# HGRN2's halving levels two at a time, both heads of a pair at the same steps, from copied queries

## The chip, the cores and the metric

One NeuronCore of one Trainium2 chip runs the whole program; the other cores are idle. The metric is the device time of one execution, in microseconds (us): 1566.15 us, the median of 3 runs (1566.15 to 1567.37). Lower is better.

The core has five engines with a program each: TensorE (PE, matrix products), VectorE (DVE), ScalarE (ACT), GpSimd (POOL) and SyncE (SP, which starts the loads). Each takes its instructions in the order in which they stand, and they wait for each other by semaphores. PEld is TensorE's loading of weights, beside its products.

## The reference, cut to what matters

The model has two layers, on 512 tokens of 1024 channels. The first mixes tokens by HGRN2, the second by Mamba-2; after each comes a gated feed-forward with a short convolution. The change touches HGRN2 alone: for each of 8 heads of 128 channels and in both directions it computes a gated recurrence.

```python
def gla_chunked(q, k, v, logf):
    """S_t = diag(f_t) S_{t-1} + k_t v_t^T, o_t = S_t^T q_t"""
...
def hgrn2_mixer(u, w_in, lb, norm_w, w_out):
    q, f_fw, f_bw, iv, g = jnp.split(u @ w_in, 5, axis=-1)
    f = lb + (1.0 - lb) * jax.nn.sigmoid(fr)      # k = 1 - f, logf = log(f)
    q = heads(jax.nn.silu(q))
    o = gla_chunked(q, k_fw, iv, logf_fw) + flip(gla_chunked(flip(q), flip(k_bw), flip(iv), flip(logf_bw)))
    o = rmsnorm(o, norm_w) * jax.nn.silu(heads(g))
    return o.reshape(bsz, seq, HG_DIM) @ w_out
```

The weight with which token s enters the output of token t is the product of the gates between them, channel by channel, so it is no plain matrix product.

## The kernel before, in words

Channels lie on the 128 partitions and tokens along the free side, in 4 blocks of 128. All products of weights and activations are split in halves of fewer bits (`whi`, `wlo` of the weights, `uhi`, `ulo` of the activations) and made of three matmuls each (`mm3`, lines 161 to 163). SP loads a piece of weights, ACT rounds it to `whi` (line 135), DVE makes the rest `wlo` (line 136).

**The stream of projections.** `fill` projects the heads in four pairs: `q`, forward gate, backward gate, `v` and `g`, 16 units of work each, where a unit is about three matmuls of 512 columns. After the pairs follows `ao0`, the output product over the first six heads.

**The heads' own work.** `mix(hd)` is a generator for one head. In `kq` it keeps four 512-wide arrays: forward keys KF, backward queries QB, forward queries QF, backward keys KB. The token pairs within a block of 128 are taken by halving: at level m (1, 2, 4, 8, 16, 32, 64) the two neighbouring runs of m tokens meet. Up to m=16 a level gathers the keys that it needs into `km` (ACT, line 558) and makes 16 small products of 32x32 (`strips`, line 541) into a PSUM tile; a masked copy (DVE, line 566; for m=1 an ACT copy, line 563, and a masked copy of the diagonal, line 564, whose product has the sum `ks` of both keys, line 547, as weights) takes them into `atd`. At m=32 there are 16 products of 32x32 (line 572) and at m=64 8 of 64x64 (lines 580, 582). After each level three DVE instructions carry the gates one level up: two in place in `kq` (lines 594, 595: the later halves get one product of gates, the earlier halves the other), and one for the next products of gates `tot` (line 597). So a level's products must be done before `kq` is changed, and the next level needs the change. Then the keys are transposed (line 606), states between blocks are made (614, 619), the output is made (632), normed (636 to 641), transposed back (645), gated by `g` (647) and split (648, 649).

**What sets the order.** `weave` runs the stream and, when its count of units has come to a head's time, one step of that head's generator. A head has 13 steps, spread evenly over its span in `HEADS` by `HSTEPS`; the spans of neighbouring heads overlap, each with its own times. TensorE's instructions stand in just that order (`manual_schedule`). The order of DVE and ACT is made by the framework's scheduler from the dependencies, when the program is built. Buffers that the change touches: `q` and `g` 3, `km` 2, `y` 1, `kq` 2; PSUM has 3 tiles for the stream (`pp`) and 5 for the rest (`pm`).

Of the kernel before, what the change touches and what calls it, by code (L numbers as in the profile page):

```python
# [14 lines left out]
ALU = mybir.AluOpType  # L15
# [3 lines left out]
P = 128  # L19
Q = 32  # L20
T = 512
NB = T // P
# [8 lines left out]
NFF = DFF // P  # L31
FHALF = (12, 10)

HEADS = ((66, 136), (90, 170), (133, 209), (169, 250), (213, 292), (248, 315), (293, 353), (314, 368))
HSTEPS = (1, 1, 2, 3, 4, 5, 6, 7, 8.3, 9.5, 10, 11, 12)

MAMBA = [(c[0], int(c[1:])) for c in "p0 z0 p1 z1 p2 z2 o1 p3 o1 z3 o2 p4 z4 o2 p5 z5 o2 p6 z6 p7 z7 o8".split()]

# [13 lines left out]
def view(ap, offset, dims):  # L52

    return bass.AP(tensor=ap.tensor, offset=ap.offset + offset, ap=[ap.ap[0], *dims])
# [3 lines left out]
def tile_trunk(ctx: ExitStack, tc: tile.TileContext, x, norm1_w, norm2_w, a_w_in, a_lb_logits, a_norm_w, a_w_out,  # L58
# [3 lines left out]
    V, A, G, PE = nc.vector, nc.scalar, nc.gpsimd, nc.tensor  # L62
# [9 lines left out]
    def misc_ps():  # L72
        return ps.tile([P, T], F32, tag="pm", name="pm", bufs=5)
# [17 lines left out]
    masks = {}  # L91
# [187 lines left out]
    for step in MAMBA:  # L279
        g = step[1]  # L280
# [7 lines left out]
        else:  # L288
            for n in range(g):
                k, c = min(nout // 4 * 2, 6), nout % 4  # L290
# [118 lines left out]
    with tc.manual_schedule(engines={mybir.EngineType.PE, mybir.EngineType.DVE, mybir.EngineType.Activation}):  # L409
# [9 lines left out]
        w = halves(*raws[0])  # L419
# [8 lines left out]
        w = halves(*raws[2])  # L428
# [4 lines left out]
        w = halves(*raws[1])  # L433
# [4 lines left out]
        w = halves(*raws[3])  # L438
# [18 lines left out]
    def hgrn2():  # L457
# [5 lines left out]
        def t2k(tag, bufs, name=None):  # L463
            return pool.tile([P, T], F32, tag=tag, name=name or tag, bufs=bufs)
# [3 lines left out]
        def proj_pair(j):  # L468
            q, F = [], []
            if j > 0:  # L470
                wq = take(("a", j, 0))
            for i in range(2):
                if j == 0:
                    p = first[i]
                else:
                    p = proj_ps()
                    yield from proj_ch(p, wq, i * P)
                t = t2k("pr", 2)
                V.tensor_tensor(t, p, rbc, ALU.mult)
                s = t2k("sg_", 1)  # L480
                A.activation(s, t, AF.Sigmoid)
                q.append(t2k("q", 3))
                V.tensor_tensor(q[i], t, s, ALU.mult)
                F.append(pool.tile([P, 2, T], F32, tag="F", name="F", bufs=2))

            def gate(i, dr, w, p=None):
                if p is None:
                    p = proj_ps()
                    yield from proj_ch(p, w, i * P)
                t = t2k("pr", 2)  # L490
                V.tensor_tensor(t, p, rbc, ALU.mult)
                A.activation(t, t, AF.Sigmoid)
                hd = 2 * j + i
                V.tensor_scalar(F[i][:, dr, :], t, olb[:, hd:hd + 1], lb[:, hd:hd + 1], ALU.mult, ALU.add)
# [12 lines left out]
            for c in range(2):  # L507
                p = proj_ps()
                yield from proj_tok(p, wv, (2 * c, 2 * c + 1))
                for b in range(2):  # L510
                    A.activation(v[:, 2 * c + b, :], p[:, b * 256:(b + 1) * 256], AF.Copy,
                                 scale=rtok[:, 2 * c + b:2 * c + b + 1])
            wg = take(("a", j, 4))
            for i in range(2):
                p = proj_ps()
                yield from proj_ch(p, wg, i * P)
                t = t2k("pr", 2)
                V.tensor_tensor(t, p, rbc, ALU.mult)
                s = t2k("sg_", 1)
                A.activation(s, t, AF.Sigmoid)  # L520
                g.append(t2k("g", 3))
                V.tensor_tensor(g[i], t, s, ALU.mult)

        def mix(hd):
            q, F, v, g = heads[hd]
# [11 lines left out]
            def strips(lhs, rhs, p):  # L537

                for b in range(NB):
                    for j in range(0, P, Q):  # L540
                        PE.matmul(p[j:j + Q, b * Q:(b + 1) * Q], lhs(b * P + j), rhs(b * P + j), start=True, stop=True)

            def pq(p):
                return p[:, 0:P].rearrange("p (a b) -> p a b", b=Q)

            ks = t2k("km", 2)
            V.tensor_tensor(ks, kq[:, KF, :], kq[:, KB, :], ALU.add)
            p0 = misc_ps()
            strips(lambda o: ks[:, o:o + Q], lambda o: q[:, o:o + Q], p0)
            yield  # L550
            tot = F
            m = 1
            while m < P:
                n2 = T // (2 * m)
                pl = misc_ps()
                if m < Q:
                    km = t2k("km", 2)
                    A.copy(km.rearrange("p (a b c) -> p a b c", b=2, c=m),
                           view(kq, 0, [[2 * m, n2], [3 * T + m, 2], [1, m]]))
                    strips(lambda o: km[:, o:o + Q],  # L560
                           lambda o: view(kq, T + o, [[2 * m, Q // (2 * m)], [T + m, 2], [1, m]]), pl)
                    if m == 1:
                        A.copy(atd, pq(pl))
                        V.copy_predicated(atd, bmask(masks[0]), pq(p0))
                    else:
                        V.copy_predicated(atd, bmask(masks[m]), pq(pl))
                elif m == Q:

                    half = ((0, KF, QF, Q), (Q, KB, QB, 0), (2 * Q, KF, QF, 3 * Q), (3 * Q, KB, QB, 2 * Q))
                    for b in range(NB):  # L570
                        for j, k, r, t in half:
                            PE.matmul(pl[j:j + Q, b * Q:(b + 1) * Q], kq[:, k, b * P + j:b * P + j + Q],
                                      kq[:, r, b * P + t:b * P + t + Q], start=True, stop=True)
                    for j, k, r, t in half:
                        A.copy(pv(at0[j:j + Q])[:, :, t:t + Q], pq(pl)[j:j + Q])
                    for j in range(0, P, Q):
                        V.tensor_copy(pv(at0[j:j + Q])[:, :, j:j + Q], atd[j:j + Q])
                else:
                    for b in range(NB):
                        PE.matmul(pl[0:64, b * P + 64:b * P + 128], kq[:, KF, b * P:b * P + 64],  # L580
                                  kq[:, QF, b * P + 64:b * P + 128], start=True, stop=True)
                        PE.matmul(pl[64:128, b * P:b * P + 64], kq[:, KB, b * P + 64:b * P + 128],
                                  kq[:, QB, b * P:b * P + 64], start=True, stop=True)
                    A.copy(pv(at0[0:64])[:, :, 64:128], pv(pl[0:64])[:, :, 64:128])
                    A.copy(pv(at0[64:128])[:, :, 0:64], pv(pl[64:128])[:, :, 0:64])

                w = T // m

                def tv(half):
                    return view(tot, half, [[w, 2], [2, n2], [0, m]])  # L590

                qk2 = view(kq, QF * T + m, [[T, 2], [2 * m, n2], [1, m]])
                kq1 = view(kq, 0, [[T, 2], [2 * m, n2], [1, m]])
                V.tensor_tensor(qk2, qk2, tv(0), ALU.mult)
                V.tensor_tensor(kq1, kq1, tv(1), ALU.mult)
                nt = pool.tile([P, 2, n2], F32, tag=f"tot{m}", name=f"tot{m}", bufs=2 if m > 2 else 1)
                V.tensor_tensor(nt, view(tot, 0, [[w, 2], [2, n2]]), view(tot, 1, [[w, 2], [2, n2]]), ALU.mult)
                tot = nt
                m *= 2
                yield  # L600

            kt, blocks = [], ((0, 1, 2), (3, 2, 1))
            for a, bl in zip((KF, KB), blocks):
# [17 lines left out]
                for n, b in enumerate(bl):  # L621
                    states[dr, b + 1 - 2 * dr] = sd[:, n, :]
            yield
            yield

            po = misc_ps()
            for t in range(NB):
# [15 lines left out]
            pt = misc_ps()  # L643
            for t in range(NB):
                PE.transpose(pt[:, t * P:(t + 1) * P], on[:, t * P:(t + 1) * P], ident)
            y = t2k("y", 1)
            V.scalar_tensor_tensor(y, pt, col(W_AN, 0), g[i], ALU.mult, ALU.mult)
            A.copy(yhi[hd], y)
            V.tensor_tensor(ylo[hd], y, yhi[hd].bitcast(F32), ALU.subtract)
# [5 lines left out]
                yield from proj_pair(j)  # L655
            yield from out_proj("ao0", yhi[:6], ylo[:6], None)

        jobs = [(mix(i), [a + (b - a) * f / 13 for f in HSTEPS]) for i, (a, b) in enumerate(HEADS)]
        with tc.manual_schedule(engines={mybir.EngineType.PE}):
            weave(fill(), jobs, 32)  # L660
        run(out_proj("ao1", yhi[6:], ylo[6:], lambda d: prep(d, (W_N2[0], W_N2[1]), pool)))
# [484 lines left out]
```

## Time and profile before

| | |
|---|---|
| median of the runs | 1566.15 us |
| profiled execution, its own time | 1567.89 us |
| its span, first to last instruction | 1566.1 us |
| TensorE busy | 1544.3 us (99%) |
| VectorE busy | 1042.7 us (67%) |
| ScalarE busy | 776.9 us (50%) |
| mean granted TensorE clock | 0.995 of full |

A share of busy time says which engine is short over the whole span; a timeline row gives the start, the time of the (merged) instructions, engine, line, operation and tiles, and in brackets how long the engine was idle before it and who ended that. Matmul records overlap: a record is longer than the step to the next one. A 32x32 product of full precision leaves two records, so 16 products are a row of x32. The granted clock is given in shares of full speed, 2.4 GHz; 0.50 is the lower level, 1.2 GHz.

### The profile page before, as it was taken

The numbers are of one execution on the slowest core, as the hardware profiler recorded it, in microseconds if no ns is written. First come the engines' busy times: TensorE is split into PE (matmuls) and PEld (weight loads), VectorE is DVE, ScalarE is ACT, GpSimd is POOL, SyncE is SP. The second block draws the span as 40 slices with busy tenths as digits, with TensorE's granted clock in tenths as the row PEclk, the third lists the DMA queues.
The fourth block names the chain that finished last, engine by engine and source line by source line (L and its number), as shares of the span: only waits on it lengthen the run. The fifth ranks groups of instructions, "written<-read, shape, count | busy, mean of one in ns | idle before, by whom it ended". The sixth has DMA issues, their size and how long they took to land.

```text
span 1566.1 us, 24651 instructions
## 1 busy us (share of the span) xinstructions
PE 1544.3 (99%) x9959; PEld 1287.7 (82%) x9959; DVE 1042.7 (67%) x1675; ACT 776.9 (50%) x1382; POOL 27.2 (2%) x31
## 2 busy tenths in 40 slices
PE   8999999999999999999999999999999999999998
PEld 6878788887888888887887888888887888888887
DVE  6687778758664346645988887778978655346543
ACT  5445545435333223333698886667845333123333
POOL 0000000000000000000000000000000000000000
PEclk9999999999999999999999999999999999999999
DMA  5322221113232332323443433333313323233221
GB/s 181 95 69 69 69 82 62 56 49 127 88 108 81 108 96 93 101 88 91 129 125 114 142 103 113 122 103 114 101 48 123 106 82 107 81 108 101 81 86 70
DMA packets 153592, 151.52 MB, mean 97 GB/s; under 512 B 8374, under 2 KB 144263, under 8 KB 153479
## 3 DMA queue, kind: packets, MB, share of 16 engines
q1 hardware_dynamic: 153415, 149.93, 30.8%
q8 instruction: 78, 1.28, 0.3%
q14 instruction: 35, 0.29, 0.1%
q0 software_dynamic: 32, 0.02, 0.0%
q10 hardware_dynamic: 32, 0.01, 0.0%
HBM read 147.70 MB, written 2.23 MB: 96 GB/s over the span
## 4 chain that ended last, share of the span: by engine, by line
PE 49%; DVE 2%; ACT 1%; issue 1%; POOL 0%; POOLq 0%; ACTq 0%
PE pp L161 14%; PE pp L163 14%; PE pp L162 14%; PE pm L960 2%; PE pm L954 1%; PE pm L921 1%; PE pm L870 0%; PE pm L994 0%; PE pm L881 0%; PE pm L163 0%; PE pm L161 0%; PE pm L162 0%; PE pm L865 0%; PE pm L1075 0%; ACT whi L135 0%
## 5 line engine op out<-in xcount | busy, mean ns | idle before, releaser
L161 PE MATMUL pp<-uhi,whi 128*128 128x512 f32 x1184 | 474.7, 401 | 0.0
L163 PE MATMUL pp<-uhi,wlo 128*128 128x512 f32 x1184 | 462.6, 391 | 0.3 <-DVE wlo L136 0.3
L162 PE MATMUL pp<-ulo,whi 128*128 128x512 f32 x1184 | 462.7, 391 | 0.0
L135 ACT CAST whi<-raw 128x1024 fp32r<-128x1024 f32 (+1 forms) x258 | 260.0, 1008 | 318.4 <-PE pp L162 246.2
L136 DVE TENSOR_TENSOR wlo<-raw,whi 128x1024 fp32r<-128x1024 f32 (+1 forms) x258 | 301.5, 1170 | 152.6 <-ACT whi L135 151.8
L163 PEld LDWEIGHTS pp<-uhi,wlo 128*128 128x128 f32 x1184 | 222.8, 188 | 48.9 <-DVE wlo L136 1.2
L161 PEld LDWEIGHTS pp<-uhi,whi 128*128 128x128 f32 x1184 | 223.1, 188 | 46.1 <-issue 0.5
L162 PEld LDWEIGHTS pp<-ulo,whi 128*128 128x128 f32 x1184 | 223.3, 189 | 45.0 <-issue 0.8
L161 PE MATMUL pp<-yh,whi 128*128 128x512 f32 (+1 forms) x500 | 197.2, 394 | 0.9 <-ACT whi L135 0.9
L163 PE MATMUL pp<-yh,wlo 128*128 128x512 f32 (+1 forms) x500 | 191.8, 384 | 0.0
L162 PE MATMUL pp<-yl,whi 128*128 128x512 f32 (+1 forms) x500 | 190.7, 381 | 0.0
L161 PE MATMUL pp<-whi,uhi 128*128 128x256 f32 x384 | 111.3, 290 | 0.0
L163 PEld LDWEIGHTS pp<-yh,wlo 128*128 128x128 f32 x500 | 93.8, 188 | 20.3
L161 PEld LDWEIGHTS pp<-yh,whi 128*128 128x128 f32 x500 | 94.0, 188 | 18.9 <-ACT whi L135 1.3
L162 PEld LDWEIGHTS pp<-yl,whi 128*128 128x128 f32 x500 | 93.9, 188 | 18.8
L255 DVE TENSOR_TENSOR h<-h,pp 128x512 f32<-128x512 f32 x80 | 54.3, 685 | 81.6 <-PE pp L163 80.9
L163 PE MATMUL pp<-whi,ulo 128*128 128x256 f32 x384 | 108.6, 283 | 0.0
L162 PE MATMUL pp<-wlo,uhi 128*128 128x256 f32 x384 | 108.5, 283 | 0.0
L899 ACT ACTIVATE E<-R,col_t 128x128 f32<-128x128 f32 x256 | 81.4, 392 | 27.8 <-PE pm L954 21.9
L679 ACT ACTIVATE c<-gp,colp 128x512 f32<-128x512 f32 x44 | 35.8, 817 | 98.0 <-DVE gp L677 98.0
L681 DVE SCALAR_TENSOR_TENSOR c<-gp,colp,c 128x512 f32<-128x512 f32 x88 | 65.6, 750 | 20.8 <-ACT c L679 19.4
L161 PEld LDWEIGHTS pp<-whi,uhi 128*128 128x128 f32 x384 | 73.4, 191 | 0.9
(277 smaller groups left out, 1882.0 us busy)
## 6 DMA issues: line engine op xcount, KB each, us to landing
raw<-in_ffn_w_in_dram SPq DMA_DIRECT2D x88, 512.0 KB, 3.5
raw<-in_a_w_in_dram SPq DMA_DIRECT2D x40, 512.0 KB, 3.6
raw<-in_ffn_w_out_dram SPq DMA_DIRECT2D x40, 512.0 KB, 3.4
raw<-in_b_w_in_dram SPq DMA_DIRECT2D x32, 512.0 KB, 3.8
R<-ac_d SPq DMA_DIRECT2D x64, 256.0 KB, 3.8
raw<-in_b_w_in_dram SPq DMA_DIRECT2D x32, 256.0 KB, 3.3
raw<-in_b_w_out_dram SPq DMA_DIRECT2D x12, 512.0 KB, 3.4
xt<-in_x_dram SPq DMA_DIRECT2D x4, 512.0 KB, 8.5
```

The costliest lines, as they stand in the source:

```text
L135: A.copy(hi[:, :nk, :c0], r)
L136: V.tensor_tensor(lo[:, :nk, :c0], r, hi[:, :nk, :c0].bitcast(F32), ALU.subtract)
L161: PE.matmul(dst, lhi, rhi, start=start, stop=False)
L162: PE.matmul(dst, lhi, rlo, start=False, stop=False)
L163: PE.matmul(dst, llo, rhi, start=False, stop=stop)
L255: V.tensor_tensor(h[d], h[d], p, ALU.add)
L679: A.activation(c, g[:, 0:T], AF.Identity, scale=col(W_FW[l], f), bias=col(W_FB, l * NFF + f))
L681: V.scalar_tensor_tensor(c, g[:, k:k + T], col(W_FW[l], k * NFF + f), c, ALU.mult, ALU.add)
L899: A.activation(e[:, bs], r[:, bs], AF.Identity, bias=col_t[:, b, dr * NH + hd:dr * NH + hd + 1])
L921: PE.matmul(dst, b_t[:, dr + c, :], xds[dr][:, c, :], start=True, stop=True)
L954: PE.matmul(py[b // 2][i:i + 64, o:o + 64], w[:, b * P + i:b * P + i + 64], x_t[:, b, j * 64:(j + 1) * 64], start=True, stop=True)
L960: PE.matmul(po[:, i * 256:(i + 1) * 256], sc[:, c * P:(c + 1) * P], hin[dr][:, c - 1 if dr == 0 else c, :], start=True, stop=True)
```

## The change

Each head now goes through its levels in four steps instead of eight, and the two heads of a pair take those four at the same times. Step 1 makes the diagonal and level 1; step 2 levels 2 and 4; step 3 levels 8 and 16; step 4 levels 32 and 64. Within a step both levels' products go into one PSUM tile. So that level m's products can wait for those of level 2m, its keys and now its queries too are copied first (`keys`, `queries`, on ACT), then `kq` is carried up (`widen`, the old three DVE instructions), then the keys of 2m are copied. `both` runs the step of head a, then that of head b. The rest of a head's work (transposes, states, output, end) takes four more steps at the times in `ENDS`.

```diff
-HEADS = ((66, 136), (90, 170), (133, 209), (169, 250), (213, 292), (248, 315), (293, 353), (314, 368))
-HSTEPS = (1, 1, 2, 3, 4, 5, 6, 7, 8.3, 9.5, 10, 11, 12)
+PAIRS = (66, 138, 214, 289)
+LEVELS = (5, 18, 32, 45)
+ENDS = ((50, 55, 62, 67), (56, 61, 67, 73))
...
+            def keys(m):
+                km = t2k("km", 4)
+                A.copy(km.rearrange("p (a b c) -> p a b c", b=2, c=m),
+                       view(kq, 0, [[2 * m, T // (2 * m)], [3 * T + m, 2], [1, m]]))
+                return lambda o: km[:, o:o + Q]
+            def queries(m):
+                qm = t2k("qm", 2)
+                A.copy(qm.rearrange("p (a b c) -> p a b c", b=2, c=m),
+                       view(kq, T, [[2 * m, T // (2 * m)], [T + m, 2], [1, m]]))
+                return lambda o: qm[:, o:o + Q]
+            def widen(tot, m):
...
+            ks = t2k("km", 4)
+            V.tensor_tensor(ks, kq[:, KF, :], kq[:, KB, :], ALU.add)
+            km = keys(1)
+            pl = misc_ps()
+            strips(lambda o: ks[:, o:o + Q], lambda o: q[:, o:o + Q], pl[:, 0:P])
+            strips(km, lambda o: view(kq, T + o, [[2, Q // 2], [T + 1, 2], [1, 1]]), pl[:, P:2 * P])
+            A.copy(atd, pq(pl[:, P:2 * P]))
+            V.copy_predicated(atd, bmask(masks[0]), pq(pl[:, 0:P]))
+            tot = widen(F, 1)
+            for m in (2, 8):
+                km, qm = keys(m), queries(m)
+                tot = widen(tot, m)
+                km2 = keys(2 * m)
                 yield
+                pl = misc_ps()
+                strips(km, qm, pl[:, 0:P])
+                strips(km2, lambda o: view(kq, T + o, [[4 * m, Q // (4 * m)], [T + 2 * m, 2], [1, 2 * m]]),
+                       pl[:, P:2 * P])
+                for i2, n in enumerate((m, 2 * m)):
+                    V.copy_predicated(atd, bmask(masks[n]), pq(pl[:, i2 * P:(i2 + 1) * P]))
+                tot = widen(tot, 2 * m)
+            for j in range(0, P, Q):
+                V.tensor_copy(pv(at0[j:j + Q])[:, :, j:j + Q], atd[j:j + Q])
+            km, qm = keys(Q), queries(Q)
+            tot = widen(tot, Q)
+            yield
+            pl = misc_ps()
...
+            tot = widen(tot, 2 * Q)
+            yield
...
-            y = t2k("y", 1)
+            y = on
...
+        def both(a, b):
+            for _ in LEVELS:
+                next(a)
+                next(b)
+                yield
+        jobs = []
+        for j, t in enumerate(PAIRS):
+            ab = [mix(2 * j + i) for i in range(2)]
+            jobs.append((both(*ab), [t + f for f in LEVELS]))
+            jobs += [(m, [t + f for f in e]) for m, e in zip(ab, ENDS)]
```

`q` and `g` have 2 buffers instead of 3, `km` 4 instead of 2, `qm` 2. In the changed program line numbers are larger: 161 to 163 are 162 to 164, 135 and 136 are 136 and 137, 541 is 542, 547 is 577, 558 is 550 (keys) and 556 (queries), 563 and 564 are 582 and 583, 594, 595 and 597 are 569, 570 and 572.

On TensorE, at the first levels of pair 0. In these rows `pm` is a PSUM tile of the heads and `pp` one of the stream; `kq_692` and `q_464` are those of head 0 and `q_471` that of head 1; `kq_971` before and `kq_752` now are head 1's. Before, head 1's first products (head 0's stand 84 rows ahead, in a place of their own):

```order
L163 MATMUL pp_964<-uhi1_84,wlo_807 128x512
L541 MATMUL pm_980<-q_471,km_978 32x32 x16
L541 MATMUL pm_997<-kq_971,km_998 32x32 x16
L161 MATMUL pp_964<-uhi2_85,whi_806 128x512
L162 MATMUL pp_964<-ulo2_93,whi_806 128x512
```

Now:

```order
L164 MATMUL pp_667<-uhi7_90,wlo_550 128x512
L542 MATMUL pm_703<-q_464,km_699 32x32 x16
L542 MATMUL pm_703<-kq_692,km_701 32x32 x16
L542 MATMUL pm_763<-q_471,km_759 32x32 x16
L542 MATMUL pm_763<-kq_752,km_761 32x32 x16
L162 MATMUL pp_818<-uhi0_83,whi_543 128x512
```

The two heads' first four sets of products now stand right behind each other; head 1's have moved from a place of their own to the place of head 0's.

On VectorE, around the sum of head 1's keys (`km_978` before, `km_759` now). `tot` are the products of gates, `F` the gates themselves, `pr` and `g` belong to the stream. Before:

```order
L566 COPY_PREDICATED atd_698<-m8_184,pm_865 128x128
L594 TENSOR_TENSOR kq_692<-kq_692,tot4_851 128x64x8
L595 TENSOR_TENSOR kq_692<-kq_692,tot4_851 128x64x8
L483 TENSOR_TENSOR q_893<-pr_889,sg__891 128x512
L547 TENSOR_TENSOR km_978<-kq_971 128x512
L597 TENSOR_TENSOR tot64_1436<-tot32_1358 128x8
L136 TENSOR_TENSOR wlo_955<-raw_952,whi_954 128x1024
L566 COPY_PREDICATED atd_698<-m16_187,pm_915 128x128
```

Now:

```order
L569 TENSOR_TENSOR kq_692<-kq_692,F_466 128x512
L583 COPY_PREDICATED atd_698<-m0_176,pm_703 128x128
L570 TENSOR_TENSOR kq_692<-kq_692,F_466 128x512
L523 TENSOR_TENSOR g_816<-pr_812,sg__814 128x512
L569 TENSOR_TENSOR kq_692<-kq_692,tot1_740 128x256x2
L570 TENSOR_TENSOR kq_692<-kq_692,tot1_740 128x256x2
L572 TENSOR_TENSOR tot1_800<-F_473 128x512
L577 TENSOR_TENSOR km_759<-kq_752 128x512
L569 TENSOR_TENSOR kq_752<-kq_752,F_473 128x512
```

The sum for head 1 stood among head 0's later levels; it now stands behind two rounds of carrying up of head 0, which follow head 0's first products.

On ScalarE, the copies of keys and queries at the same place. Before, from the copy of head 0's level-1 products to its second next copy of keys:

```order
L563 COPY atd_698<-pm_718 128x128
L558 COPY km_769<-kq_692 128x512
L135 CAST whi_806<-raw_804 128x1024
L135 CAST whi_812<-raw_810 128x1024
L558 COPY km_830<-kq_692 128x512
```

Now:

```order
L582 COPY atd_698<-pm_703 128x128
L550 COPY km_742<-kq_692 128x512
L556 COPY qm_744<-kq_692 128x512
L550 COPY km_750<-kq_692 128x512
L550 COPY km_761<-kq_752 128x512
L582 COPY atd_758<-pm_763 128x128
L550 COPY km_802<-kq_752 128x512
L556 COPY qm_804<-kq_752 128x512
```

Keys and queries of level 2 and the keys of level 4 of head 0 now stand ahead of head 1's level-1 keys (`km_761`).

## Rows read from the trace of the kernel before

**Rows 1.** The page, part 1: busy time, share of the span, instructions.

```profile
PE 1544.3 (99%) x9959; PEld 1287.7 (82%) x9959; DVE 1042.7 (67%) x1675; ACT 776.9 (50%) x1382; POOL 27.2 (2%) x31
```

**Rows 2.** Who waited for whom, TensorE, the whole run: total us, times, longest us.

```profile
PE pm L954 <- DVE E L903: 4.1, 2, 3.4
PE pm L240 <- DVE dg L238: 3.4, 2, 3.1
...
PE pm L541 <- DVE km L547: 0.7, 1, 0.7
```

**Rows 3.** Busy time by stretch, from the first to nearly the last of the heads' work (columns: stretch, length, busy time and instructions of each engine, granted clock, DMA share, GB/s).

```profile
68.90:360.00 291.10, 288.97 (x3325) 238.32 (x3324) 217.57 (x419) 145.03 (x330) 8.17 (x8) 1.00 0.22 69
```

**Rows 4.** Timeline of TensorE at a place with one set of 16 products, and at a place with two.

```profile
78.34 0.39 PE L163 MATMUL pp<-uhi,wlo 128*128 128x512 f32 x1
78.66 0.46 PE L541 MATMUL pm<-kq,km 128*32 128x32 f32 x32
79.05 0.50 PE L161 MATMUL pp<-uhi,whi 128*128 128x512 f32 x1
79.38 0.39 PE L162 MATMUL pp<-ulo,whi 128*128 128x512 f32 x1
79.61 0.40 PE L163 MATMUL pp<-uhi,wlo 128*128 128x512 f32 x1
...
89.70 0.39 PE L163 MATMUL pp<-uhi,wlo 128*128 128x512 f32 x1
90.02 0.46 PE L541 MATMUL pm<-q,km 128*32 128x32 f32 x32
90.30 0.56 PE L541 MATMUL pm<-kq,km 128*32 128x32 f32 x32
90.79 0.50 PE L161 MATMUL pp<-uhi,whi 128*128 128x512 f32 x1
91.12 0.39 PE L162 MATMUL pp<-ulo,whi 128*128 128x512 f32 x1
```

**Rows 5.** Timeline of VectorE behind head 0's first products, which end on TensorE at 69.72 (start 69.16 and 0.56).

```profile
69.75 0.69 DVE L594 TENSOR_TENSOR kq<-kq,F 128x512 f32<-128x512 f32 x1
70.53 0.31 DVE L564 COPY_PREDICATED atd<-m,pm 128x128 f32<-128x128 uint8 x1
70.74 0.69 DVE L595 TENSOR_TENSOR kq<-kq,F 128x512 f32<-128x512 f32 x1
71.34 0.69 DVE L522 TENSOR_TENSOR g<-pr,sg__745 128x512 f32<-128x512 f32 x1
```

**Rows 6.** Timeline of TensorE and ScalarE there and, last, of ScalarE at two instructions behind each other.

```profile
69.16 0.56 PE L541 MATMUL pm<-kq,km 128*32 128x32 f32 x32
...
71.46 0.70 ACT L558 COPY km<-kq 128x512 f32<-128x512 f32 x1 [0.96 <-DVE kq L595]
...
52.74 0.85 ACT L558 COPY km<-kq 128x512 f32<-128x512 f32 x1
53.50 0.63 ACT L492 ACTIVATE pr<-pr 128x512 f32<-128x512 f32 x1
```

**Rows 7.** The instructions by line and shape, from 0 to 420 us (columns: line, engine, operation, out<-in, shapes, count | busy us, mean ns of one | idle before).

```profile
L136 DVE TENSOR_TENSOR wlo<-raw,whi 128x1024 fp32r<-128x1024 f32 x57 | 69.7, 1223 | 33.7 <-ACT whi L135 33.1
L594 DVE TENSOR_TENSOR kq<-kq,tot 128x512 f32<-128x512 f32 x48 | 32.9, 686 | 0.3 <-PE pm L572 0.2
L558 ACT COPY km<-kq 128x512 f32<-128x512 f32 x40 | 27.4, 684 | 40.9 <-DVE kq L595 36.2 <-DVE kq L532 2.8 <-PE pm L541 1.9
L566 DVE COPY_PREDICATED atd<-m,pm 128x128 f32<-128x128 uint8 x32 | 9.5, 297 | 5.6 <-PE pm L541 5.5
L597 DVE TENSOR_TENSOR tot<-F 128x512 f32<-128x512 f32 x8 | 5.5, 690 | 0.1
L547 DVE TENSOR_TENSOR km<-kq 128x512 f32<-128x512 f32 x8 | 5.5, 684 | 0.0
```

**Rows 8.** Timeline of VectorE and TensorE at the one place where TensorE waited for the sum of the keys.

```profile
235.57 0.68 DVE L595 TENSOR_TENSOR kq<-kq,tot 128x512 f32<-128x512 f32 x1
236.17 0.69 DVE L547 TENSOR_TENSOR km<-kq 128x512 f32<-128x512 f32 x1
...
237.00 0.43 PE L541 MATMUL pm<-q,km 128*32 128x32 f32 x29 [0.74 <-DVE km L547]
```

**Rows 9.** Busy time by stretch, as in rows 3: the two stretches of lower clock inside the run.

```profile
33.68:40.50 6.82, 6.23 (x13) 4.23 (x14) 3.69 (x12) 3.65 (x6) 0.00 (x0) 0.50 0.00 1
...
835.81:842.64 6.83, 5.80 (x27) 4.74 (x28) 6.83 (x11) 5.81 (x16) 0.00 (x0) 0.50 0.73 204
```

**Rows 10.** Timeline of TensorE at these two: the first instruction behind the idle time, and steps of the stream at the lower clock.

```profile
34.27 2.08 PE L240 MATMUL pm<-dg,ones 128*128 128x512 f32 x2 [3.10 <-DVE dg L238]
...
37.85 0.63 PE L162 MATMUL pm<-ulo,whi 128*128 128x512 f32 x1
38.28 0.63 PE L163 MATMUL pm<-uhi,wlo 128*128 128x512 f32 x1
38.71 0.63 PE L161 MATMUL pp<-uhi,whi 128*128 128x512 f32 x1
...
836.84 1.12 PE L954 MATMUL pm<-xt,E 128*64 128x64 f32 x16 [3.37 <-DVE E L903]
```

More of the change, by code (lines that the diff above doesn't have):

```diff
@@ L481, in proj_pair @@
                 A.activation(s, t, AF.Sigmoid)
-                q.append(t2k("q", 3))
+                q.append(t2k("q", 2))
                 V.tensor_tensor(q[i], t, s, ALU.mult)
@@ L520, in proj_pair @@
                 A.activation(s, t, AF.Sigmoid)
-                g.append(t2k("g", 3))
+                g.append(t2k("g", 2))
                 V.tensor_tensor(g[i], t, s, ALU.mult)
@@ L543, in pq @@
             def pq(p):
[L544 to L587, printed above, removed]
@@ new lines, in pq @@
+                return p.rearrange("p (a b) -> p a b", b=Q)
+            def keys(m):
[8 more added lines that the diff above has]
+                return lambda o: qm[:, o:o + Q]
@@ L589, in tv @@
+            def widen(tot, m):
+                n2, w = T // (2 * m), T // m
                 def tv(half):
@@ L597, in mix @@
                 V.tensor_tensor(nt, view(tot, 0, [[w, 2], [2, n2]]), view(tot, 1, [[w, 2], [2, n2]]), ALU.mult)
-                tot = nt
-                m *= 2
-                yield
+                return nt
+            ks = t2k("km", 4)
[4 more added lines that the diff above has]
+            strips(km, lambda o: view(kq, T + o, [[2, Q // 2], [T + 1, 2], [1, 1]]), pl[:, P:2 * P])
@@ new lines, in mix @@
+            for j in range(0, P, Q):
[4 more added lines that the diff above has]
+            pl = misc_ps()
+            for b in range(NB):
+                for j in range(0, P, Q):
+                    t = b * P + (j ^ Q)
+                    PE.matmul(pl[j:j + Q, t:t + Q], km(b * P + j), qm(t), start=True, stop=True)
+            for b in range(NB):
+                PE.matmul(pl[0:64, b * P + 64:b * P + 128], kq[:, KF, b * P:b * P + 64],
+                          kq[:, QF, b * P + 64:b * P + 128], start=True, stop=True)
+                PE.matmul(pl[64:128, b * P:b * P + 64], kq[:, KB, b * P + 64:b * P + 128],
+                          kq[:, QB, b * P:b * P + 64], start=True, stop=True)
@@ L602, in mix @@
+            for j in range(0, P, Q):
+                t = j ^ Q
+                A.copy(pv(at0[j:j + Q])[:, :, t:t + Q], pv(pl[j:j + Q])[:, :, t:t + Q])
+            A.copy(pv(at0[0:64])[:, :, 64:128], pv(pl[0:64])[:, :, 64:128])
+            A.copy(pv(at0[64:128])[:, :, 0:64], pv(pl[64:128])[:, :, 0:64])
+            tot = widen(tot, 2 * Q)
+            yield
             kt, blocks = [], ((0, 1, 2), (3, 2, 1))
@@ L623, in mix @@
             yield
-            yield
             po = misc_ps()
@@ L656, in fill @@
             yield from out_proj("ao0", yhi[:6], ylo[:6], None)
-        jobs = [(mix(i), [a + (b - a) * f / 13 for f in HSTEPS]) for i, (a, b) in enumerate(HEADS)]
+        def both(a, b):
[8 more added lines that the diff above has]
+            jobs += [(m, [t + f for f in e]) for m, e in zip(ab, ENDS)]
         with tc.manual_schedule(engines={mybir.EngineType.PE}):
```

## The prediction, before the run

> **What bounds the kernel now.** I read the page's busy times first [rows 1]: TensorE works in 99% of the span, VectorE in 67%, ScalarE in half. The list of who waited for whom [rows 2] says the same from the other side: over the whole run TensorE's longest waits are two of 3.1 and 3.4 us, both outside the heads' work. Then the stretch that holds nearly all of that work, 68.90 to 360 us [rows 3]: TensorE 288.97 of 291.10 us, VectorE 217.57 (75%), ScalarE 145.03, clock full throughout. So there the time is the sum of what TensorE is given. A change wins only by giving it less or cheaper work; it loses by every wait that it puts into TensorE's order, for the stream's matmuls stand behind the waiting one and can't pass it.
>
> **What is removed.** The number of products is the same. What goes are places at which the stream is broken. At a place with one set of 16 small products the stream's matmul at 78.34 and the second one behind the place, at 79.38, lie 1.04 us apart [rows 4]; two plain steps (79.38 to 79.61) would be 0.46, so the place costs 0.58. With two sets it is 89.70 to 91.12, so 1.42 - 0.46 = 0.96. A set is 0.38, breaking in costs 0.20. Before, a head breaks in 7 times for levels (1 with the diagonal, 2, 4, 8, 16, 32, 64): 56, less one where two stand together. Now 4 per pair: 16. Saved: 39 x 0.20 = 7.8 us. Bounds: 5.4, if in the last step, where 32x32 and 64x64 products take turns, each of three changes is a new break (12 x 0.20 less); 9.8, if some ten places of transposes, states and outputs that are now joined save as much. I take 7.8.
>
> **What is added on ScalarE.** Four more copies per head (queries at 2, 8 and 32, keys at 32), 32 x 0.684 us [rows 7] = 22 us, on an engine that is idle for 146 of 291 us [rows 3]: nothing by itself. One fewer buffer of q and g each: q is last read at a pair's first step and g at its last, both well before the stream makes the next but one: nothing. That cover would be gone if a pair ran some 15 units late, and then the stream's DVE copy would hold `pp`.
>
> **The wait that is added.** It is in the first step of each pair. TensorE's rows there (order of the changed kernel, above) are: diagonal and level 1 of head a, then at once the same of head b, whose diagonal needs b's sum of keys (`km_759`, L577). In VectorE's order that sum stands behind eight instructions, the first of which (L569, carrying a up by level 1) must wait for a's products, since it overwrites what they read; and the fifth (L569 with `tot1`) waits for ScalarE's copies of a's keys and queries, which wait for the third. So TensorE, having done a's half, waits for a chain through three engines before it may do b's. Along the rows of before, where the first links stand just so: a's products end at 69.72 [rows 6]; the first carry starts at 69.75, the masked copy and the second carry at 70.74 [rows 5]; the copy of the keys on ScalarE at 71.46, 0.70 long [rows 6]. The query copy, of the same shape, starts 0.09 before that ends (as 53.50 stands to 52.74 plus 0.85), at 72.07, and ends at 72.77. VectorE goes on about 0.1 later, at 72.87, with four instructions 0.60 apart (70.74 to 71.34): two carries, the product of gates, the sum, which starts at 74.67 and takes 0.68 [rows 7], to 75.35. From there to TensorE it was 0.14 the one time that TensorE waited for this sum (236.86 to 237.00) [rows 8], so b's products start at 75.49: 5.8 us of idle TensorE. The stream's `g` or a `wlo` of 1.22 us [rows 7] that stands between lies under ScalarE's two copies. b's level-1 keys (`km_761`), behind the keys of level 4 in ScalarE's order, come at about 75.7, when the diagonal's 0.28 us of products [rows 4] are through: no more. Bounds of one wait: 5.4 with every link at its issue step and no hop, 6.4 with the full means of rows 7 and four hops of 0.14. All four pairs have the same order: 4 x 5.8 = 23.2 us, all on the path, for TensorE has nothing else in front.
>
> **What the wait does to the clock.** The run of before holds two idle times of this kind. TensorE stopped at 31.17 for 3.10 us and at 833.47 for 3.37 [rows 10]. The granted clock fell to 0.50, which is 1.2 GHz, at 33.68 and at 835.81, 2.5 and 2.3 us after the stop, each time for 6.83 us, of which TensorE worked 6.23 and 5.80 [rows 9]. In it the stream's step is 0.43 instead of 0.23 [rows 4, 10], so 0.47 of the time is lost: 2.9 and 2.7 us. A wait of 5.8 us is longer than both, so I expect the fall at each of the four. Bounds for one: 1.6, if the stretch begins 2.4 us after the stop, so that 3.4 us of it are left behind the wait; 4.8, if the long idle time brings a second stretch behind the first (10.3 us x 0.47); zero, if the clock holds, which no row of so long an idle time shows. I take the rows' middle, 2.8: 4 x 2.8 = 11.2 us.
>
> The Trainium skill, TensorE: Matmul & The Clock Gate, section "HAM oscillation — how this bites in real kernels", tells of a kernel that waits between bursts of matmuls, and whose every burst then starts at the lower clock, at a price of half the slowed time. By that rule the price would be paid at each of the four waits and be 3.1 instead of 2.9 us for the first row; the trace agrees with it twice out of two.
>
> **The later steps.** Between steps 2 and 3 TensorE has 42 stream matmuls and four sets, 42 x 0.23 + 0.20 + 4 x 0.38 = 11.4 us; VectorE has four masked copies at 0.2, eight carries at 0.60 [rows 5], two small `tot`, one `pr` and one `wlo`: 0.8 + 4.8 + 0.7 + 0.6 + 1.2 = 8.1, and ScalarE's last copy of keys behind them, 0.7. It fits by some 2 us, and by 1 where only 36 stream matmuls lie between (10.0). I count nothing; if each of the 12 gaps were 1 us late, 12 us more.
>
> **Sum.** -7.8 + 23.2 + 11.2 = +26.6 us, against the profiled execution's own 1567.89: 1594.5. That execution is 1.74 above the median of the runs, 1566.15, so I predict 1592.7.
>
> **Rivals.**
> - The wait comes, the clock holds: -7.8 + 23.2 = +15.4, so 1581.5. For it: nothing but that no idle time of just this length stands in the trace. Against: both of 3 us and over made the clock fall. 14%.
> - VectorE becomes the bound at the later steps as well: 12 gaps late by 1 us or so on top, 1604.7. For it: 75% busy on average [rows 3], and the levels are the densest part. Against: the sums above. 11%.
> - The other side: TensorE does not wait to speak of, and the 39 places are won: 1558.3. The mechanism would be b's sum of keys made before a's first products end, as it was before, where it stood far ahead and cost 0.74 us once [rows 8]. It decides the sign at 7.8 / 4 = 1.95 us per pair, clock included. Against: the order on VectorE, which is in the program, not in chance. 4%.
> - The forecast, wait and clock: 71%.
>
> A measurement of this kernel can tell about 0.2% (3 us) from no change. Faster 0.04, same 0.01, slower 0.95. The range reaches from the case of the clock that holds, with short waits (1566.15 - 9.8 + 4 x 5.4 = 1578), to four waits of 6.4 with the long price of the clock at two of them: 1566.15 - 7.8 + 25.6 + 5.6 + 9.6 = 1599, and some of the later steps: 1606.
>
> **What would show it.** Right: in the list of TensorE's waits the line of the small products (L542) waiting for VectorE's sum (L577), four times, 5 to 6.5 us each, and behind each a stretch of clock 0.50 of about 7 us; a place with four sets at about 1.7 us; no wait of TensorE over 1 us at steps 2 to 4. Wrong: L542 idle less than 2 us before the third set of a first step; a clock of 1.00 right behind the waits; TensorE waiting for `km` or `qm` of L550 and L556 in steps 2 to 4, which would be the second rival.

## The result and the profile after

The changed kernel takes 1586.55 us (median of 4 runs, 1583.42 to 1588.49) against 1566.15 for the kernel before; the ratio is 1.0131, with a 95% interval of 1.0119 to 1.0144. The change makes the kernel slower by 20.4 us. The forecast was 1592.7, so +26.6.

The page's busy times, which answer to [rows 1]:

```profile
PE 1541.9 (97%) x9959; PEld 1297.0 (82%) x9959; DVE 1041.7 (66%) x1675; ACT 794.3 (50%) x1414; POOL 27.9 (2%) x31
```

TensorE has as many instructions as before and 2.4 us less busy time, in a span that is 19.0 us longer (1585.1). So no work was added; the loss shows as waiting, and what a lower clock adds to the busy time is hidden in it behind what the joined places save (taken apart under the first experiment). Who waited for whom on TensorE, the whole run (total us, times, longest us), beside [rows 2]:

```profile
PE pm L542 <- DVE km L577: 22.1, 4, 5.7
...
PE pm L663 <- ACT on L659: 1.5, 2, 1.0
```

The first row is new: the small products wait four times for VectorE's sum of keys. The place is each pair's first step. This is the timeline of TensorE, VectorE and ScalarE at pair 0, the chain that the prediction put together from [rows 4 to 6]:

```profile
66.07 0.56 PE L542 MATMUL pm<-kq,km 128*32 128x32 f32 x32
66.67 0.69 DVE L569 TENSOR_TENSOR kq<-kq,F 128x512 f32<-128x512 f32 x1
67.65 0.68 DVE L570 TENSOR_TENSOR kq<-kq,F 128x512 f32<-128x512 f32 x1
68.37 0.69 ACT L550 COPY km<-kq 128x512 f32<-128x512 f32 x1 [0.96 <-DVE kq L570]
68.96 0.66 ACT L556 COPY qm<-kq 128x512 f32<-128x512 f32 x1
69.66 0.69 DVE L569 TENSOR_TENSOR kq<-kq,tot 128x512 f32<-128x512 f32 x1 [0.72 <-ACT qm L556]
70.27 0.69 DVE L570 TENSOR_TENSOR kq<-kq,tot 128x512 f32<-128x512 f32 x1
70.99 1.36 ACT L550 COPY km<-kq 128x512 f32<-128x512 f32 x2 [1.36 <-DVE kq L570]
71.60 0.69 DVE L577 TENSOR_TENSOR km<-kq 128x512 f32<-128x512 f32 x1
72.34 0.65 PE L542 MATMUL pm<-q,km 128*32 128x32 f32 x32 [5.70 <-DVE km L577]
73.94 0.63 PE L163 MATMUL pp<-ulo,whi 128*128 128x512 f32 x1
74.37 0.63 PE L164 MATMUL pp<-uhi,wlo 128*128 128x512 f32 x1
```

Read it from the end: TensorE starts head b's products at 72.34, when the sum (71.60) is done; the sum stands behind the carry-up of head a, which stands behind ScalarE's two copies, which stand behind head a's first carry-up, which waits for head a's products (end 66.63). The last two rows are the stream, in steps of 0.43 instead of 0.23. The other three waits end at 145.57 (5.39 long), 224.23 (5.51) and 299.83 (5.51).

The stretches of lower clock, busy time by stretch, beside [rows 9]:

```profile
69.81:76.64 6.83, 4.30 (x72) 3.57 (x73) 4.22 (x8) 2.88 (x5) 0.00 (x0) 0.50 0.01 2
144.90:151.73 6.83, 6.16 (x76) 5.04 (x77) 3.40 (x7) 2.82 (x5) 0.00 (x0) 0.50 0.15 52
223.41:230.24 6.83, 6.01 (x87) 5.95 (x88) 4.25 (x8) 3.40 (x6) 0.00 (x0) 0.50 0.01 2
298.50:305.33 6.83, 5.50 (x85) 5.44 (x86) 4.06 (x7) 3.80 (x8) 0.00 (x0) 0.50 0.01 2
```

Each begins inside a wait and lasts 6.83 us; TensorE works 4.30 to 6.16 us of it.

What the change does gain stands in the timeline of TensorE at a place with four sets, beside [rows 4]:

```profile
82.94 0.39 PE L164 MATMUL pp<-uhi,wlo 128*128 128x512 f32 x1
83.26 0.46 PE L542 MATMUL pm<-qm,km 128*32 128x32 f32 x32
83.53 0.47 PE L542 MATMUL pm<-kq,km 128*32 128x32 f32 x31
...
83.83 0.46 PE L542 MATMUL pm<-qm,km 128*32 128x32 f32 x30
...
84.13 0.48 PE L542 MATMUL pm<-kq,km 128*32 128x32 f32 x31
84.54 0.50 PE L162 MATMUL pp<-uhi,whi 128*128 128x512 f32 x1
84.87 0.39 PE L163 MATMUL pp<-ulo,whi 128*128 128x512 f32 x1
```

82.94 to 84.87 less two plain steps is 1.93 - 0.46 = 1.47 us for four sets, where four places with one set took 4 x 0.58 = 2.32.

### The profile page after: what moved, and what is told of

The parts are those of the page before. It is cut to its first block, busy times and chain, and to the rows that moved or that the text cites. A ratio compares the mean times of both kernels' runs of the same rounds, so it can differ in the third digit from the quotient of the medians.

```text
span 1585.1 us, 24676 instructions
## 1 busy us (share of the span) xinstructions
PE 1541.9 (97%) x9959; PEld 1297.0 (82%) x9959; DVE 1041.7 (66%) x1675; ACT 794.3 (50%) x1414; POOL 27.9 (2%) x31
## 4 chain that ended last, share of the span: by engine, by line
PE 50%; DVE 1%; ACT 1%; issue 1%; POOL 0%; POOLq 0%; ACTq 0%
PE pp L162 14%; PE pp L164 14%; PE pp L163 14%; PE pm L989 2%; PE pm L983 1%; PE pm L950 1%; PE pm L899 0%; PE pm L1023 0%; PE pm L910 0%; PE pm L163 0%; PE pm L162 0%; PE pm L164 0%; PE pm L894 0%; PE pm L1104 0%; ACT whi L136 0%
## 5 line engine op out<-in xcount | busy, mean ns | idle before, releaser
L162 PEld LDWEIGHTS pp<-whi,uhi 128*128 128x128 f32 x384 | 75.7, 197 | 0.6
```

What stands on the lines that cost most here:

```text
L162: PE.matmul(dst, lhi, rhi, start=start, stop=False)
```

## The experiments

Each was timed in five rounds beside the kernel before on the same chip, and its ratio is to those runs of before (medians 1565.30 to 1565.72 us). The stage is the time from the first small product to the next norm's sums of squares (L227, later L228): it holds the heads' work, and leaves out how the start of an execution happened to go.

| kernel | median us | ratio to before (95%) | stage us |
|---|---|---|---|
| before | 1566.15 | | 302.54 |
| the change | 1586.55 | 1.0131 (1.0119 to 1.0144) | 324.42 |
| e1 both heads' keys first | 1555.04 | 0.9939 (0.9927 to 0.9951) | 292.69 |
| e2 the sum in a tile of its own | 1587.90 | 1.0144 (1.0131 to 1.0158) | 324.84 |
| e4 TensorE busy in the wait | 1578.33 | 1.0086 (1.0072 to 1.0099) | 316.00 |
| e5 levels in twos, heads apart | 1564.82 | 1.0002 (0.9993 to 1.0011) | 301.91 |
| e8 the same, keys early | 1558.14 | 0.9953 (0.9941 to 0.9966) | 295.66 |
| e6 e1, level-1 queries copied | 1558.91 | 0.9958 (0.9945 to 0.9972) | 295.78 |
| e7 e1, last step later | 1562.57 | 0.9981 (0.9972 to 0.9989) | 299.93 |
| e10 e1, all ends earlier | 1559.13 | 0.9959 (0.9946 to 0.9973) | 295.00 |
| e9 e1, ends apart | 1552.94 | 0.9918 (0.9905 to 0.9932) | 289.96 |

### Both heads' keys before either's products

```diff
             km = keys(1)
+            yield
             pl = misc_ps()
...
         def both(a, b):
+            next(a)
+            next(b)
             for _ in LEVELS:
```

> Head b's sum of keys and its level-1 keys are emitted before head a's first products, so that all four keys of a pair's first step are ready before the step; nothing else changes. My theory (each pair's wait is head b's keys queued behind head a's carry-up): no wait of TensorE before the small products of a first step, granted clock 1.00 in the heads' stretch, and only the won places are left, 10.4 us by the accounts of the changed kernel's trace: 1566.15 - 10.4 = 1555.8, within 1553 to 1559. Rival 1 (VectorE is the real bound, the sum is only where it shows): the waits move to the third set or to steps 2 to 4, and the time is 1566 or more. Rival 2 (the places are worth the 7.8 us of the prediction): 1558.3.

Measured: 1555.04 us. TensorE's waits from 60 to 400 us, and busy time in the stage:

```profile
PE pm L664 <- ACT on L660: 1.5, 2, 1.0
PE pp L162 <- DVE h L256: 1.1, 1, 1.1
```

```profile
68.08:360.77 292.69, 290.17 (x3373) 248.36 (x3372) 226.00 (x434) 168.59 (x373) 8.84 (x8) 1.00 0.24 72
```

No wait is left before any small product, not at steps 2 to 4 either, and the clock is 1.00. So VectorE is not the bound, although it was busy for 13.84 us of the 14.00 between 76 and 90. The same stretch of the changed kernel and of the kernel before shows where the 21.9 us of the change come from:

```profile
65.80:390.22 324.42, 299.79 (x3373) 256.80 (x3372) 228.03 (x435) 170.10 (x374) 8.83 (x8) 0.96 0.21 65
```

```profile
68.88:371.42 302.54, 300.26 (x3373) 247.19 (x3373) 228.99 (x435) 152.93 (x342) 8.17 (x8) 1.00 0.22 70
```

With the same 3373 products TensorE is busy for 300.26 us before and 290.17 in e1: joined places save 10.1. In the changed kernel it is busy for 299.79: the same sets of products, in four first places torn in two by the wait and at the lower clock behind it, cost 9.6 more (the run with TensorE busy in the wait parts the two). And it is idle for 324.42 - 299.79 = 24.6 instead of 2.3: 22.4 us of waits. -10.1 + 22.4 + 9.6 = +21.9.

### Only the wait that the list names

```diff
-            ks = t2k("km", 4)
+            ks = at0
```

> Only the wait that the list of waits names is taken away: the sum of keys goes into the head's own free tile at0 instead of one of the four km buffers, so that head b's sum has no buffer to wait for; in the program it now stands early on VectorE, as it did before the change. Head b's level-1 keys still stand on ScalarE behind head a's keys of level 4. My theory (the whole preparation of b is late, and the sum is only the last of it): head b's first set goes at once, and its second waits for the keys of L550, 5.0 to 5.8 us in each pair; the clock falls as before; 1583 to 1589. Rival (the sum is the cause): no wait, 1556 to 1559.

Measured: 1587.90 us, no gain. TensorE's waits and the timeline at pair 0:

```profile
PE pm L542 <- ACT km L550: 22.5, 4, 6.4
```

```profile
66.03 0.47 PE L542 MATMUL pm<-q,at 128*32 128x32 f32 x31
...
70.59 1.36 ACT L550 COPY km<-kq 128x512 f32<-128x512 f32 x2 [1.36 <-DVE kq L570]
...
72.00 0.66 PE L542 MATMUL pm<-kq,km 128*32 128x32 f32 x32 [5.50 <-ACT km L550]
```

Head b's first set now goes at once (66.03), and the second waits as long for ScalarE. The merged pair of copies at 70.59 is head a's level 4 and head b's level 1, in that order. So the named releaser was only the last of two that came at about the same time, as the prediction's end of the chain said (sum through at 75.35, level-1 keys at about 75.7). In the changed program head b's sum and level-1 keys take over the buffers of head a's, since head a alone fills all four `km` buffers in its first step. With the sum elsewhere a buffer is free at pair 0 for head b's level-1 keys, and the scheduler still orders them behind head a's. Why it does was not pursued; only emitting both first (e1) moved them. Whether more `km` buffers alone would do it was not tried.

### TensorE busy in the wait

```diff
                 next(a)
+                if n == 0:
+                    pd = misc_ps()
+                    for _ in range(20):
+                        PE.matmul(pd, uhi[0][:, 0:P], uhi[0], start=True, stop=True)
                 next(b)
```

> Adds work whose result nobody reads: between head a's and head b's first step TensorE gets 20 products of 512 columns, 20 x 0.23 = 4.6 us, which lie inside the wait of 5.4 to 5.7 us. My theory (the clock falls because TensorE stands still in the wait, and that costs 10.3 us): the third set still starts when b's sum is ready, so the waits shrink to about 1 us each and nothing is gained there; the clock stays at 1.00 and 10.3 us go: about 1576, within 1574 to 1579. Rival (the low clock behind the waits costs nothing, or comes from something else): 1586.5. If the products lengthen the step, more than 1586.5.

Measured: 1578.33 us, 8.2 less than the change. TensorE's waits, its timeline at pair 0 and the busy time there:

```profile
PE pm L542 <- DVE km L577: 3.4, 4, 1.0
```

```profile
67.66 4.84 PE L683 MATMUL pm<-uhi 128*128 128x512 f32 x20
73.45 0.46 PE L542 MATMUL pm<-q,km 128*32 128x32 f32 x32 [0.96 <-DVE km L577]
73.73 0.56 PE L542 MATMUL pm<-kq,km 128*32 128x32 f32 x32
74.22 0.50 PE L162 MATMUL pp<-uhi,whi 128*128 128x512 f32 x1
```

```profile
66.00:80.00 14.00, 13.04 (x178) 10.33 (x177) 9.38 (x15) 6.76 (x12) 0.00 (x0) 1.00 0.11 37
```

Head b's products start 6.56 us behind head a's first (66.89), as in the change (65.80 to 72.34, 6.54). Nothing is won in the chain, yet the clock stays at 1.00 and the stage is 8.4 us shorter. So the fall comes from standing still, and 8.4 us is its price by this run. The 9.6 of e1 holds something else beside it. These are the first of the four sets and the stream behind them in e1:

```profile
68.08 0.46 PE L542 MATMUL pm<-q,km 128*32 128x32 f32 x32
69.48 0.50 PE L162 MATMUL pp<-uhi,whi 128*128 128x512 f32 x1
```

There the four sets take 1.40 us. In the change head a's two end 0.83 behind their start (65.80 to 66.63), and head b's two, at full clock, take 0.77 to the stream (73.45 to 74.22, here). So a place torn in two by the wait costs 0.2 more, 0.8 over four pairs, and 8.8 of the 9.6 are left for the clock. What I had missed in part: at the lower clock head b's two sets and the way to the stream took 72.34 to 73.35, 1.01, against 0.77 here: a quarter of that time is lost, not the 0.47 that the stream loses.

### One half of the change: levels in twos, each head at its own times

```diff
+HEADS = ((66, 136), (90, 170), (133, 209), (169, 250), (213, 292), (248, 315), (293, 353), (314, 368))
+HSTEPS = (1, 3, 5, 7, 8.3, 9.5, 11, 12)
...
+        jobs = [(mix(i), [a + (b - a) * f / 13 for f in HSTEPS]) for i, (a, b) in enumerate(HEADS)]
```

> Half of the change: levels two at a time from copied queries, but each head at its own times (the spans of the kernel before), with 3 km and 3 g buffers. There is no second head behind the first products, so no wait at L542 by my theory. Places: per head 4 instead of 7. By the prices read in the changed kernel's trace (0.30 us for breaking in, 0.28 us for a set, 0.38 for the strided one of level 1, 1.26 for levels 32 and 64 together) a head costs 0.96 + 2 x 0.86 + 1.26 = 3.94 instead of 4.72: 8 x 0.78 = 6.2 us won, 1560, within 1557 to 1563. Rival 1 (breaking in is worth the prediction's 0.20): 8 x 3 x 0.20 = 4.8, 1561.4. Rival 2 (doubling the levels is what makes TensorE wait, not the pairing): waits for km or qm appear, 1566 or more.

Measured: 1564.82 us, the same as before: a miss by 5. Timeline of VectorE and TensorE at head 1's first step:

```profile
88.78 0.68 DVE L568 TENSOR_TENSOR kq<-kq,tot 128x512 f32<-128x512 f32 x1
89.39 0.68 DVE L569 TENSOR_TENSOR kq<-kq,tot 128x512 f32<-128x512 f32 x1
89.99 0.68 DVE L576 TENSOR_TENSOR km<-kq 128x512 f32<-128x512 f32 x1
90.72 0.46 PE L541 MATMUL pm<-q,km 128*32 128x32 f32 x32 [3.31 <-DVE km L576]
```

The same wait, without a second head in the step: head 1's sum stands behind head 0's carry-up of its third step. It came here at 90.72 (3.31 us) and at 299.81 (2.07). Behind the first the clock fell, when TensorE was at work again:

```profile
91.44:94.85 3.41, 3.41 (x19) 2.68 (x9) 2.09 (x5) 1.52 (x3) 0.00 (x0) 0.50 0.13 42
```

The two waits and the lower clock took back what the places had won. That joining the heads makes the wait was too narrow; a sum that is emitted in the very step that needs it can come to stand behind another head's carry-up, and did here in two of eight first steps (in the kernel before once, for 0.74 us [rows 8]). The next run asks whether that is all:

```diff
-HSTEPS = (1, 3, 5, 7, 8.3, 9.5, 11, 12)
+HSTEPS = (0, 1, 3, 5, 7, 8.3, 9.5, 11, 12)
...
-            ks = t2k("km", 3)
+            ks = at0
...
             km = keys(1)
+            yield
```

> As e5_levels_alone, but each head's sum of keys and level-1 keys are emitted 1/13 of its span (4 to 6 units) before its first products, the sum in at0. In e5_levels_alone two first steps waited for the sum, 3.3 and 2.1 us, and the clock fell behind the first. My theory (those two waits and the fall are all that hid the 6.2 us of the places): no wait at L541 and about 1559, within 1557.5 to 1560.5; so doubling the levels alone is worth 6 and putting the two heads together another 4. Rival (single heads' doubled steps are too short for VectorE): waits for km or qm at later steps, 1563 or more.

Measured: 1558.14 us, with no wait for the sum and one of 0.6 us for `km`. Levels in twos alone shorten the stage by 6.9 us, and e1, with the heads together, is 3.0 shorter still (292.69). A place with two sets in its timeline:

```profile
74.48 0.39 PE L163 MATMUL pp<-uhi,wlo 128*128 128x512 f32 x1
74.80 0.46 PE L541 MATMUL pm<-qm,km 128*32 128x32 f32 x32
75.07 0.49 PE L541 MATMUL pm<-kq,km 128*32 128x32 f32 x32
75.49 0.50 PE L161 MATMUL pp<-uhi,whi 128*128 128x512 f32 x1
75.82 0.40 PE L162 MATMUL pp<-ulo,whi 128*128 128x512 f32 x1
```

75.82 - 74.48 - 0.46 = 0.88 us, where the place of [rows 4], which holds the diagonal and level 1, took 0.96.

### The strided queries of level 1

```diff
-            km = keys(1)
+            km, qm = keys(1), queries(1)
...
-            strips(km, lambda o: view(kq, T + o, [[2, Q // 2], [T + 1, 2], [1, 1]]), pl[:, P:2 * P])
+            strips(km, qm, pl[:, P:2 * P])
```

> As e1_sums_first, but head's level-1 queries are copied too (one more ScalarE copy per head), so that the fourth and second set of a first step read a plain row instead of single elements two apart. Tells why the prediction's set was 0.38 and not 0.28 us. My theory (the strided query operand costs about 0.1 us per set of 16 at level 1): the record of the level-1 set falls from 0.56 to about 0.47, the first place from 1.60 to about 1.42 to 1.48; 8 sets x 0.1 = 0.8 us less than e1_sums_first, 1554.2. Rival (the difference is the place in the order, not the operand): the record and the place stay at 0.56 and 1.60; 1555.0. If ScalarE's copies come late, a wait for qm at L542 and more than 1556.

Measured: 1558.91 us. The place did as expected (pair 0's first place 1.48 instead of 1.59 us, the last record of the set 0.48 instead of 0.55), and the time went the other way: TensorE's waits in the heads' last step (L664, for ScalarE's scaled copies) grew from 1.5 to 3.8 us. Around the longest of them (1.97 us):

```profile
193.43 0.68 DVE L569 TENSOR_TENSOR kq<-kq,F 128x512 f32<-128x512 f32 x1
197.56 0.16 DVE L656 TENSOR_SCALAR ss<-ss 128x4 f32<-128x4 f32 x1
199.07 1.14 ACT L660 ACTIVATE on<-pm,rs 128x128 f32<-128x128 f32 x4 [1.82 <-POOL rs L658]
```

ScalarE is idle there for 1.82 us (0.90 in e1). With the queries copied, the next pair's first carry-up (L569, then L570) need no longer wait for that pair's products, and on VectorE it now stands ahead of the norm's step (L656), which comes 1.97 us behind the start of the squares instead of 1.27. In one other place (0.80 us) the added copy itself stands before the squares. 0.06 us per set are not worth that.

### The ends

The remaining waits of e1 are in the last step. Three settings of `ENDS` were tried on it:

```diff
-ENDS = ((50, 55, 62, 67), (56, 61, 67, 73))
+ENDS = ((50, 55, 62, 69), (56, 61, 67, 75))
```

> As e1_sums_first, but the last step of each head (transposing the output back) comes two units of the stream later. In e1_sums_first TensorE waits there twice for ScalarE's scaled copies, 1.5 us together, and the four places of b's last step cost 0.44, 0.44, 0.97 and 2.15 us, those of a's with b's output 2.67, 2.69, 2.77 and 3.76 where 0.44 + 2.24 = 2.68 is plain. My theory (these are waits for the norm's chain over VectorE, GpSimd and ScalarE, which two units more cover): all last steps cost 0.44, 1.5 to 3.4 us won, 1552 to 1553.5. Rival (the chain is late because ScalarE is behind the next pair's work, and the wait moves along): 1555 as before.

Measured: 1562.57 us; the waits of L664 are 5.7 us instead of 1.5, and the clock fell behind two of the four, of 1.43 and 2.35 us. A step put later waits longer: head b's squares (L655) stand on ScalarE behind head a's rounded output (L667), which waits for head a's end. In three of the four places they wait for still more, the remainder of head a's output (L668):

```profile
196.96 0.28 ACT L655 ACTIVATE on<-pm 128x128 f32<-128x128 f32 x1 [1.12 <-DVE ylo L668]
```

The squares write `on`, which has one buffer, and since the change head a's end keeps its output in it (`y = on`). Then the other way:

```diff
+ENDS = ((48, 53, 59, 64), (54, 59, 66, 73))
```

> As e1_sums_first, with other times of the heads' last four steps: a's output and its transposing back three units earlier, b's output one unit earlier, so that a's end no longer stands in one place with b's output. e7_later_ends showed that a later end makes the wait for ScalarE's scaled copies longer, not shorter (5.7 us instead of 1.5), because head b's squares stand on ScalarE behind head a's rounded output, which waits for a's end. My theory (the wait goes when a's end is done before b's output): the last steps cost 0.44 each, the 1.5 us of waits go and with them up to 3.4 us of places, 1552 to 1554. Rival (ScalarE's order brings the next pair's copies in between all the same): 1555 or more.

```diff
+ENDS = ((48, 53, 59, 64), (53, 58, 64, 70))
```

> As e1_sums_first, with all of the heads' last four steps two to three units earlier, a's end in one place with b's output as there. Tells whether it is the next pair's preparation on ScalarE that makes b's end late. My theory: b's chain is then over before that preparation begins, and the waits of L664 go from 1.5 us to under 0.5: 1553 to 1554.5. Rival (the chain is bound to a's end as in e9's theory): 1555 as e1_sums_first.

Measured: e9 1552.94, e10 1559.13. TensorE's waits in e9 from 60 to 400 us are a single row:

```profile
PE pp L162 <- DVE h L256: 1.1, 1, 1.1
```

All eight last places cost 0.44 to 0.45 us there. In e10 no wait is listed at head b's ends, as its theory had it, but three are at head a's (1.1 us together), and the four transposes there take 1.10 us instead of 0.60, since the scaled copies come one by one. ScalarE stands idle before those copies for 0.4 to 0.9 us, until GpSimd has the norm's factor (L658). That explains some of its 2.3 us over e1 in the stage, the rest stays open. e9 is the fastest kernel of the study: 12.8 us under its runs of before.

## Why the prediction was right, and where its sizes were off

The direction, the place and the mechanism are those of the forecast, each seen in the trace and switched off by a run (the wait by e1, the lower clock by e4); the measured 1586.55 us lies within its range (1578 to 1606). All three terms were off to the same side, so nothing cancelled: it is a forecast of the right mechanism with sizes some per cent to a quarter off. By its steps:

- **The wait.** Right. Counted from the end of head a's products, the prediction had the second carry at 1.02, ScalarE's copy at 1.74, VectorE again at 3.15, the sum at 4.95 and head b's products at 5.77 us; the rows above give 1.02, 1.74, 3.03, 4.97 and 5.71. Four waits are 22.1 instead of 23.2 us: the later three are 0.2 to 0.3 shorter than the first. In the third, head a's copy into `atd` (L582) starts on ScalarE as soon as its products are done (218.75), where in pair 0 it stood behind the stream's sigmoid (67.17), and all behind it comes 0.2 earlier. One count was wrong without consequence: the sum stands behind seven instructions of VectorE, not eight.
- **The lower clock.** Right in kind, four times out of four. "Four times 2.8", 11.2 us, was too much: 8.4 by e4, 8.8 by e1 without the torn places (0.8 us, which stood in no term). The stretch began 3.2 to 4.7 us behind the stop, not 2.3 to 2.5, so in pair 0 more than a third of it lay inside the wait; and the small products that come first lose a quarter, not 0.47. By the rule of the Trainium skill that the prediction weighed (TensorE: Matmul & The Clock Gate, "HAM oscillation — how this bites in real kernels"), half of the slowed work is lost: half of the 21.96 us that TensorE worked in the four stretches is 11.0. The trace agrees that each of the four waits is paid for, and makes it 8.4 to 8.8.
- **The places.** This term was mis-sized too: "A set is 0.38, breaking in costs 0.20". One set is 0.58, two are 0.88 (e8), four 1.47, so a set is 0.30 and breaking in 0.28. The two-set place of [rows 4] held the strided set of level 1, whose record is 0.56 instead of 0.46 there; its extra price went into the set and out of the breaking-in. With the measured sizes a pair saves 0.3 at step 1 (1.59 in e1 for both heads, 0.96 each apart), 2 x (4 x 0.58 - 1.47) = 1.7 at steps 2 and 3, and 0.6 at step 4 (2.20 for both heads' last levels, 0.59 and 0.81 apart), 10.4 over four pairs; 10.1 was measured, not 7.8. Its sign, a place with four sets at about 1.7, came out at 1.47.
- **The last step.** The bound said that each of three changes between 32x32 and 64x64 might be a new break of 0.20. Together they cost 0.3: 2.20 for both heads, where 0.28 for breaking in and twice (0.30 + 0.53) make 1.94 (0.53 is 0.81 less the breaking-in). The Trainium skill, TensorEngine Tiling (Array Packing), section "Key Properties", says that a change of the tiling drains TensorE; that fits a price at each change, here 0.28 on the way into a place and back, and 0.1 between the two small sizes.
- **The later steps.** "I count nothing" held: no wait at steps 2 to 4, in the change and in e1. The rival with VectorE as the bound falls.
- **The rival on the other side** was the case of e1: with head b's keys made before head a's first products end, the places are won, 1555.04 (the rival said 1558.3).
- **ScalarE's copies** cost nothing in the change beyond the two that are links of the wait's chain (68.37 to 69.62 in pair 0). In e6 one more per head did cost, most of it through what it let VectorE do earlier.
- **The profiled executions** differ by 19.0 us, less than the stage's 21.9, because the first small product came 3.1 us earlier in the one of after (65.80 and 68.88), where the start lost less time; in the eleven profiles that first product lies between 65.4 and 68.9. Behind the stage they differ by 0.2.

The terms measured: -10.1 + 22.4 + 9.6 (8.8 of it the clock, 0.8 the torn places) = +21.9 in the stage, against -7.8 + 23.2 + 11.2 = +26.6.

## What to carry to other kernels

When two chains of work are put into one step of an engine that takes its instructions in order, all that the second one needs must be made before the first one's products, not behind what follows them: a join that saves 10 us lost 32 for want of three lines of code. The list of waits names the last releaser only; taking away that one alone (e2) moved the wait to the next operand at the same price. The price of a wait is more than its length where the clock falls behind it, and busy and idle time of one stretch in three kernels split such a result into its terms.

## What the runs showed of the hardware that was not expected

- In the change the granted clock fell 3.2 to 4.7 us after TensorE stopped, where the two stops of the kernel before had shown 2.5 and 2.3. Each of the four stretches of 0.50 was 6.83 us long; those of e5 and e7 in the heads' work were 3.41.
- The length of a wait alone does not say whether the clock falls. In e7 it fell behind a wait of 1.43 us (TensorE at work again from 199.92, the fall at 200.8), while waits of 2.07 us (e5) and 1.97 us (e6) left it at 1.00.

```profile
200.80:204.21 3.41, 3.41 (x17) 3.41 (x18) 1.44 (x2) 1.70 (x4) 0.00 (x0) 0.50 0.00 0
```

- At the lower clock the sets of 32x32 products slow down less than the stream: 1.01 against 0.77 us, where the stream's step goes from 0.23 to 0.43.
- A moving operand that takes single elements in turn from two arrays (level 1's queries, each two apart in its array) makes a set of 16 products of 32x32 dearer by about 0.06 us (first place 1.59 against 1.48, two such sets).
